# Two-layer streaming encoder: the second layer's conditioning rows are summed in the stage of the first output projection, and their order is changed

## The chip, the cores and the metric

The kernel runs on one core of one Trainium2 chip. The metric is device microseconds of one execution, here the median of three: 1983.85 us, from 1979.78 to 1991.28. One execution was also profiled. It took 1989.06 us, and the profile's span, from its first to its last instruction, is 1987.3 us.

Five engines work side by side, each through its own queue in the order in which its instructions were recorded: TensorE (PE in the profile, PEld for its weight loads), VectorE (DVE), ScalarE (ACT), GpSimd (POOL) and SyncE (SP). SP issues every DMA of this kernel. An instruction that must wait holds up everything behind it on the same queue.

## The reference, cut to what matters

Two layers work on a sequence of 2048 frames of width 1024. Layer 0 mixes with an RG-LRU block, layer 1 with a gated DeltaNet. Each is conditioned by three rows of 1024 numbers, shift, scale and gate, which are sums over the rows of a 1024 x 3072 matrix, weighted by one activated vector:

```python
c_act = jax.nn.silu(c)
for i in range(DEPTH):
    cond = c_act @ ada_w[i] + ada_b[i]
    shift = cond[:, None, :D_MODEL]
    scale = cond[:, None, D_MODEL:2 * D_MODEL]
    gate = cond[:, None, 2 * D_MODEL:]
    h = rmsnorm(x, norm_g[i]) * (1.0 + scale) + shift
    ...
    x = x + gate * out
return rmsnorm(x, final_g)
```

A mixer begins with a wide projection of h and ends with an output projection to `out`. So layer 1's shift and scale are needed when its normed input is made, after layer 0's output projection; layer 1's gate is needed at the very end.

## The kernel before

**Stages.** Frames are cut into two units of 1024 (NU), each into two tiles of 512 (NTC) and each tile into four blocks of 128. The program goes through: the projections of layer 0 (called `in1`, two units of 32 jobs) with the convolution, gates and scan of the RG-LRU beside them; the output projection of layer 0 (`out1`, 16 blocks by two halves, 32 jobs); the projections of layer 1 (`in2`, two units) with the DeltaNet beside them; and the output projection of layer 1. A job is 24 matmuls of 128x128 by 128x512 into one bank (`products`, line 663): each operand is split into a high and a low part, and three products are added for each of eight slices.

**What sets the order.** The program is written by generators ("threads"), and a planner, `Weave`, steps them: a thread asks for an engine for an estimated time, for a buffer (`slots`), or for an event, and the planner lets the one go first that can start earliest, with the smaller priority number ahead at equal times. The order of its choices is the order on each queue of the chip. A buffer class hands its buffers out in turn: with two buffers of class `tt`, the third request waits until the first has been given back.

**The rows.** The first four half rows of layer 0's shift and scale are made at the start of the program. The other eight half rows, layer 0's gate and all of layer 1, are made by `row_halves_thread` (line 397). For each half row it takes one of two `tt` buffers as an accumulator, and then four times: takes one of two `raw` buffers (which the weight panels also use), issues a DMA of 512 KB (line 408, tile `araw`), and adds its two 128x512 halves on VectorE (lines 413 and 415). TensorE then sums the accumulator over the partitions into a bank `adapt`: four one-column matmuls for shift and scale (`columns_of`, line 283, then `finish_columns`, lines 274 and 277), or one 128x512 matmul for a gate (line 426), to which a row of `ada_b` is added; layer 1's gate is written to memory for later (line 443). The list of half rows, (layer, part, half) with part 0 shift, 1 scale and 2 gate, is given on line 1643, and at the end the event `gates` is set.

**Who needs them.** `split_thread` (line 559) makes one slice of the normed input: ScalarE applies scale and shift (line 565), VectorE rounds to the high part (573), VectorE or GpSimd makes the low part (579, 576). It waits for `cond` of its layer. `panels_thread` loads the third weight panel of `in2` only after `gates` (line 622).

**The output projection of layer 0.** For each job, `residual1_thread` (line 919) waits for a tile `xr` of x loaded by `xr_thread` (line 932, issued on line 939, two buffers), multiplies the bank by the gate (923), adds (925) and writes the result to `x1_d` (928; the profile calls it `x_d`). Only when that write has landed is the buffer loaded again. `y_thread` (883) loads and splits one block of the mixer's result for every two jobs.

**The turn.** Beside these jobs the first two tiles of layer 1's input are turned, eight blocks in all: `turned_thread` (520) loads a block of `x1_d` (530), `scale_thread` (448) squares it on ScalarE into a `tt` buffer (455) and scales it, `turn_thread` (503) transposes it on VectorE (509) and writes it to `xt_d` in eight DMAs (515). When all eight are written, `reload_thread` (545) brings them back as `xk` (550), eight DMAs of 512 KB, and the splits of `in2` begin.

Of the kernel before, what the change touches and what calls it, by code (L numbers as in the profile page):

```python
# [138 lines left out]
def trunk_kernel(ctx, tc, x, c, ada_w, ada_b, ada_c, norm_c, final_g, w1, cw1, cb1, gate_w, gate_b, lam, ow1,  # L139
# [91 lines left out]
    def tile_(shape, tag, name, dtype=F32):  # L231
        p, n = tags[tag]
        return pools[p].tile(shape, dtype, tag=tag, name=name, bufs=n)

    w = Weave()
    events = {}

    def ev(*key):
        return events.setdefault(key, Event())

    def put(tag, token):
        w.put(slots[tag], token)
# [154 lines left out]
    def row_halves_thread(parts):  # L397

        row = tile_([P, D], "g1", "gate0")
        yield ev("gw", 0, 2)  # L400
        for layer, part, d in parts:
            ttok = yield slots["tt"]
            acc = tile_([P, TC], "tt", "acc")
            for q in range(4):
                wtok = yield slots["raw"]
                yield "sp", 512 * KB
                raw = tile_([P, 2, TC], "raw", "araw")
                sp.dma_start(out=raw, in_=ada_w[layer, 2 * part + d, :, 2 * q:2 * q + 2, :])
                for k in range(2):
                    ck = c_col[:, 2 * q + k:2 * q + k + 1]  # L410
                    yield "dve", STT, 0.13
                    if q + k == 0:
                        dve.tensor_scalar(acc, raw[:, 0, :], ck, None, ALU.mult)
                    else:
                        dve.scalar_tensor_tensor(acc, raw[:, k, :], ck, acc, ALU.mult, ALU.add)  # L415
                put("raw", wtok)
            ptok = yield slots["tp"]
            yield "pe", 0.86
            pt = ps.tile([P, TC], F32, tag="tp", name="adapt")
            if part < 2:  # L420
                columns_of(acc, pt)
                put("tt", ttok)
                yield from finish_columns(layer, part, d, pt[:, 0:4])
                put("tp", ptok)
                continue
            pe.matmul(pt, lhsT=ones, rhs=acc, start=True, stop=True)
            if layer == 0:
                put("tt", ttok)
                sl = row[:, d * TC:(d + 1) * TC]
                n = P  # L430
            else:
                sl = acc[0:1, :]
                n = 1
            yield "sp", 256 * KB
            j = 2 * part + d
            sp.dma_start(out=sl, in_=ada_b[layer:layer + 1, j * TC:(j + 1) * TC].to_broadcast([n, TC]))
            yield "dve", 0.61
            dve.tensor_tensor(sl, pt[0:n, :], sl, ALU.add)
            put("tp", ptok)
            w.set(ev("gate", layer, d), row)  # L440
            if layer == 1:
                yield "sp", 2 * KB
                sp.dma_start(out=gate_d[:, d * TC:(d + 1) * TC], in_=sl)
                put("tt", ttok)
        w.set(ev("gates"))
# [1183 lines left out]
    with tc.manual_schedule():  # L1629
        enter("hc", "o1", "l1")  # L1630
        ada_s = tile_([P, 2, 2, KT], "ada", "ada_s")
        norm_s = tile_([P, 2, KT], "ng", "norm_s")
        in1, in2 = [("in1", u) for u in range(NU)], [("in2", u) for u in range(NU)]
        w.spawn(first_small_thread(), 0)
        w.spawn(norm_thread((in1[0], 0), 0, x, 0, "A", [], [], htag="tg"), 1)
        w.spawn(first_loads_thread(), 1)
        w.spawn(first_pe_thread(), 1)
        w.spawn(first_dve_thread(), 0)
        w.spawn(columns_thread(), 4)
        w.spawn(panels_thread(), 1)  # L1640
        w.spawn(project_thread(), 9)
        w.spawn(lru_thread(), 4)
        w.spawn(row_halves_thread([(0, 2, 0), (0, 2, 1), (1, 0, 0), (1, 0, 1), (1, 1, 0), (1, 1, 1), (1, 2, 0),
                                   (1, 2, 1)]), 8)
        w.spawn(rows_thread(), 4)
        w.spawn(norm_thread((in1[0], 1), 0, x, TC, "B", [ev("adaissue", 3)], [ev("cond", 0, 1, 0), ev("cond", 0, 0, 0)],
                            ("yh", "yh", "yl", "yl")), 2)
        w.spawn(turned_thread((in1[1], 0), 0, x, T, "C", [ev("adaissue", 3), ev("split", (in1[0], 1), KT - 1)],
                              [ev("turned", (in1[1], 1))], [ev("ada")]), TP)
        w.spawn(turned_thread((in1[1], 1), 0, x, T + TC, "A", [ev("turned", (in1[1], 0))], [ev("loaded", (in1[1], 0))], [ev("free", in1[0], 0)]), TP)  # L1650
        w.spawn(out_weights_thread(1, ow1, 0, 0.5, "B", [ev("free", in1[0], 1)], []), 3)
        w.spawn(out_weights_thread(1, ow1, 1, 0.5, "C", [ev("w", *last[1])],
                                   [ev("free", in1[1], 0)]), 3)
        w.spawn(y_thread(), 3)
        w.spawn(xr_thread(), 3)
        w.spawn(phase1_end_thread(), 0)
        x1 = [[ev("x1", q * TB + b, d) for b in range(TB) for d in range(2)] for q in range(S // TC)]
        w.spawn(turned_thread((in2[0], 0), 1, x1_d, 0, "A", x1[0], [ev("turned", (in2[0], 1))],
                              [ev("free", in1[1], 1)]), TP)
        w.spawn(turned_thread((in2[0], 1), 1, x1_d, TC, "B", x1[1] + [ev("turned", (in2[0], 0))],  # L1660
                              [ev("loaded", (in2[0], 0))], [ev("free", "out1", 0)]), TP)
        w.spawn(turned_thread((in2[1], 0), 1, x1_d, T, "A", [ev("blkload", 0, BLK)],
                              [ev("blkload", 0, NH - 1), ev("turned", (in2[1], 1))], [ev("free", in2[0], 0)]), TP)
        w.spawn(turned_thread((in2[1], 1), 1, x1_d, T + TC, "B", [ev("turned", (in2[1], 0))],
                              [ev("loaded", (in2[1], 0))], [ev("free", in2[0], 1)]), TP)
        w.spawn(heads_thread(), 0)
        w.spawn(out_weights_thread(2, ow2, 0, onorm_s, "A", [ev("w", *last[-1])],
                                   [ev("free", in2[1], 0)]), 3)
        w.spawn(out_weights_thread(2, ow2, 1, onorm_s, "B", [ev("owissue", 2, 0)],
                                   [ev("free", in2[1], 1)]), 3)  # L1670
        w.spawn(queries_end_thread(), 0)
        w.spawn(phase2_end_thread(), 0)
        w.spawn(o_loads_thread(), 3)
        w.spawn(xt_thread(), 3)
        w.run()
        early.close()
        phase.close()
# [61 lines left out]
```

## Time and profile before

| what | value |
|---|---|
| median of three runs | 1983.85 us (1979.78 to 1991.28) |
| the profiled execution, its span | 1989.06 us, 1987.3 us |
| TensorE busy | 1869.0 us, 94% of the span |
| VectorE busy | 1500.0 us, 75% |
| ScalarE, GpSimd busy | 1025.1 us (52%), 811.3 us (41%) |
| DMA | 314.33 MB, mean 158 GB/s, queue 55.5% busy |
| first and last `araw` load | issued at 115.7 and 483.5 us |

The profile is read by stage. The first matmul of `out1` runs at about 518 us, the first one of `in2` at 701 us; the stage of the first projections lies before, and everything of layer 1 behind. A view that cuts the span into windows gives for each engine the busy time and the number of instructions, then the clock granted to TensorE as a share of full speed, the mean busy share of the 16 DMA engines and GB/s.

### The profile page before, as it was taken

Reading aid. Unit: us, or ns where it says so; the run is one execution under the profiler, and the core shown is the slowest. Engines: PE = TensorE matmul, PEld = TensorE weight load, DVE = VectorE, ACT = ScalarE, POOL = GpSimd, SP = SyncE. Lnnn points to the kernel's source line nnn. Section 1 sums busy time; section 2 is a strip of 40 time slices with the busy share of each in tenths; the row PEclk is TensorE's granted clock in tenths of the full one; section 3 lists DMA queues with packets and bytes.
Section 4 is the critical chain, followed back from the end, with each engine's and each line's share of the span. In section 5 each row is a group of like instructions: output and inputs, shape, how many; then the busy total and the mean of one; then the engine's idle time right before and its main releaser. Section 6 shows DMA issues by size and latency. Waiting matters only on the chain.

```text
span 1987.3 us, 31679 instructions
## 1 busy us (share of the span) xinstructions
PE 1869.0 (94%) x10408; PEld 1520.6 (77%) x10408; DVE 1500.0 (75%) x3176; ACT 1025.1 (52%) x2453; POOL 811.3 (41%) x1439
## 2 busy tenths in 40 slices
PE   6998889999999999999998989999999999999998
PEld 3776667787787777777777777788888888878887
DVE  6788798887644566888888897778777778877654
ACT  3655567666411225455555655555655556655321
POOL 4555664444200146555555553364343335511101
PEclk9999999999999999999999999999999999999999
DMA  8355655654578724546764447455455445577751
GB/s 333 97 159 160 220 169 171 199 170 156 172 199 206 223 63 127 136 111 160 177 161 126 107 115 187 135 125 146 114 129 142 120 127 128 142 208 233 224 185 64
DMA packets 506957, 314.33 MB, mean 158 GB/s; under 512 B 370724, under 2 KB 438564, under 8 KB 506792
## 3 DMA queue, kind: packets, MB, share of 16 engines
q1 hardware_dynamic: 506792, 312.31, 55.5%
q8 instruction: 82, 1.34, 0.3%
q14 instruction: 83, 0.68, 0.1%
HBM read 211.54 MB, written 100.67 MB: 157 GB/s over the span
## 4 chain that ended last, share of the span: by engine, by line
PE 50%; DVE 20%; DMA 10%; POOL 6%; issue 5%; ACT 5%; SPq 4%; DVEq 0%; POOLq 0%; ACTq 0%
PE mm L670 25%; PE mmo L670 12%; DVE xf L718 5%; DVE tblk L1248 2%; DVE ttmp L1245 2%; PE pg L777 2%; SPq L515 1%; DMA raw<-in_w 1%; DMA pq<-q_d 1%; DVE acc L415 1%; PE pp L1365 1%; PE py L1382 1%; DMA ada<-in_ada_w 1%; PE pS L1394 1%; PE pS L1395 1%
## 5 line engine op out<-in xcount | busy, mean ns | idle before, releaser
L718 DVE SCALAR_TENSOR_TENSOR xf<-xe,cw_s,xf 128x512 f32<-128x512 f32 x384 | 327.8, 855 | 54.9 <-POOL xf L961 32.0
L652 POOL TENSOR_TENSOR wlo<-raw,whi 128x1024 fp32r<-128x1024 f32 x48 | 122.3, 2548 | 81.0 <-ACT whi L646 67.9
L733 POOL COPY carry<-xe 128x4 f32<-128x4 f32 x128 | 36.8, 287 | 249.3 <-ACT xe L730 248.4
L1245 DVE TENSOR_TENSOR ttmp<-blk,tblk 128x60 f32<-128x60 f32 (+24 forms) x496 | 121.9, 246 | 21.0 <-DMA blk<-blk_d 11.0
L1248 DVE TENSOR_TENSOR tblk<-tblk,ttmp 128x60 f32<-128x60 f32 (+24 forms) x496 | 127.3, 257 | 10.1
L646 ACT CAST whi<-raw 128x1024 fp32r<-128x1024 f32 x96 | 100.3, 1045 | 52.8 <-DMA raw<-in_w 43.5
L730 ACT COPY xe<-mm 128x512 f32<-128x512 f32 x128 | 74.1, 580 | 78.6 <-PE mm L670 77.8
L670 PE MATMUL mmo<-oh,yh 128*128 128x512 f32 x256 | 102.2, 399 | 7.3 <-DVE xr L925 6.2
L670 PE MATMUL mm<-hh_('in2', 0)_5430,wlo 128*128 128x512 f32 x256 | 105.1, 411 | 0.0
L670 PE MATMUL mm<-hl_('in2', 0)_5431,whi 128*128 128x512 f32 x256 | 105.1, 410 | 0.0
L670 PE MATMUL mm<-hl_('in2', 1)_12333,whi 128*128 128x512 f32 x256 | 104.8, 409 | 0.0
L670 PE MATMUL mm<-hh_('in2', 0)_5430,whi 128*128 128x512 f32 x256 | 104.4, 408 | 0.0
L670 PE MATMUL mm<-hh_('in2', 1)_12332,wlo 128*128 128x512 f32 x256 | 104.3, 408 | 0.0
L670 PE MATMUL mm<-hh_('in2', 1)_12512,wlo 128*128 128x512 f32 x256 | 104.1, 407 | 0.0
L670 PE MATMUL mm<-hl_('in2', 0)_5208,whi 128*128 128x512 f32 x256 | 103.6, 405 | 0.0
L670 PE MATMUL mm<-hh_('in2', 0)_5207,whi 128*128 128x512 f32 x256 | 103.4, 404 | 0.2 <-ACT xe L730 0.2
L670 PE MATMUL mm<-hh_('in2', 0)_5207,wlo 128*128 128x512 f32 x256 | 103.5, 404 | 0.0
L670 PE MATMUL mm<-hh_('in2', 1)_12512,whi 128*128 128x512 f32 x256 | 103.5, 404 | 0.0
L670 PE MATMUL mm<-hl_('in2', 1)_12513,whi 128*128 128x512 f32 x256 | 103.2, 403 | 0.0
L670 PE MATMUL mm<-hh_('in2', 1)_12332,whi 128*128 128x512 f32 x256 | 103.1, 403 | 0.0
L670 PE MATMUL mmo<-oh,yl 128*128 128x512 f32 x256 | 101.7, 397 | 1.3 <-DVE yl L899 1.3
L670 PE MATMUL mmo<-oh,oh 128*128 128x512 f32 (+1 forms) x264 | 102.1, 387 | 0.0
(325 smaller groups left out, 5857.8 us busy)
## 6 DMA issues: line engine op xcount, KB each, us to landing
raw<-in_w SPq DMA_DIRECT2D x96, 512.0 KB, 4.3
araw<-in_ada_w SPq DMA_DIRECT2D x32, 512.0 KB, 4.6
xt<-x_d SPq DMA_DIRECT2D x32, 512.0 KB, 5.1
xt_d<-xb SPq DMA_DIRECT2D x192, 64.0 KB, 2.2
xk<-xt_d SPq DMA_DIRECT2D x24, 512.0 KB, 6.1
xt<-in_x SPq DMA_DIRECT2D x16, 512.0 KB, 5.1
ada<-in_ada_w SPq DMA_DIRECT2D x16, 512.0 KB, 9.0
y_d<-tz SPq DMA_DIRECT2D x32, 256.0 KB, 3.0
```

Source lines behind the costliest of these rows:

```text
L415: dve.scalar_tensor_tensor(acc, raw[:, k, :], ck, acc, ALU.mult, ALU.add)
L515: sp.dma_start(out=dst[c_], in_=tb[32 * c_:32 * c_ + 32])
L646: act.copy(hi, raw)
L652: pool.tensor_tensor(lo, raw, f(hi), ALU.subtract)
L670: pe.matmul(pt, lhsT=lhs[a][:, k, :], rhs=rhs[b][:, k, :], start=(k == 0 and n == 0), stop=(k == KT - 1 and n == 2))
L718: dve.scalar_tensor_tensor(xf, xe[:, 1 + j:1 + j + TC], wc[:, j:j + 1], xf, ALU.mult, ALU.add)
L730: act.copy(xe[:, 4:4 + TC], pt)
L733: pool.tensor_copy(out=carry, in_=xe[:, TC:TC + 4])
L777: pe.matmul(pg, lhsT=a[:, g, :], rhs=b, start=(q == 0), stop=(q == 2))
L1245: dve.tensor_tensor(tmp, blk[:, j, j + 1:32].unsqueeze(2).to_broadcast([P, r, c_]), t[:, j, 0:c_].unsqueeze(1).to_broadcast([P, r, c_]), A ...
L1248: dve.tensor_tensor(t[:, j + 1:32, 0:c_], t[:, j + 1:32, 0:c_], tmp, ALU.subtract)
L1365: pe.matmul(pp[:, 0, :], lhsT=kc, rhs=S_, start=True, stop=True)
```

## The change

Before the first half row of layer 1, `row_halves_thread` waits for the event `lasthalves`, which `gates_thread` sets (line 765) when the last of the 32 gate steps of the RG-LRU has its buffers, about where `out1` begins. And layer 1's half rows are taken in another order: shift and scale of the first 512 columns, then those of the second, then the gate.

```diff
@@ -399,6 +399,8 @@
         row = tile_([P, D], "g1", "gate0")
         yield ev("gw", 0, 2)
         for layer, part, d in parts:
+            if layer == 1:
+                yield ev("lasthalves")
             ttok = yield slots["tt"]
             acc = tile_([P, TC], "tt", "acc")
             for q in range(4):
@@ -1640,7 +1642,7 @@
-        w.spawn(row_halves_thread([(0, 2, 0), (0, 2, 1), (1, 0, 0), (1, 0, 1), (1, 1, 0), (1, 1, 1), (1, 2, 0),
+        w.spawn(row_halves_thread([(0, 2, 0), (0, 2, 1), (1, 0, 0), (1, 1, 0), (1, 0, 1), (1, 1, 1), (1, 2, 0),
                                    (1, 2, 1)]), 8)
```

No instruction is added or taken away; every queue holds as many as before. Lines behind 402 stand two further down in the changed kernel (line 415 is 417 there, 925 is 927, and so on). What the planner makes of it is seen in the order of the queues.

**SP, late in the first projections.** Names: `raw` is a weight panel, `wlo` a kept low part read back, `y_d` a result written, `gw` gate weights. Before:

```order
L819 DMA y_d<-tz 128x512
L408 DMA araw<-in_ada_w 128x1024
L837 DMA gw<-in_gate_w 128x256
L408 DMA araw<-in_ada_w 128x1024
L610 DMA raw_3102<-in_w 128x1024
L641 DMA wlo<-wlo_d1z_1261 128x1024
L408 DMA araw<-in_ada_w 128x1024
L819 DMA y_d<-tz 128x512
```

and now, at the same two panels:

```order
L821 DMA y_d<-tz 128x512
L839 DMA gw<-in_gate_w 128x256
L612 DMA raw_3051<-in_w 128x1024
L643 DMA wlo<-wlo_d1z_1261 128x1024
L821 DMA y_d<-tz 128x512 x2
```

All 24 `araw` loads of layer 1 have left this stage.

**VectorE, in the first jobs of the output projection.** `mmo` is the job's bank, `yl` the low part of a mixer block. Before, four jobs read:

```order
L923 TENSOR_TENSOR mmo<-mmo,gate_138 128x512
L925 TENSOR_TENSOR xr<-mmo,xr 128x512
L899 TENSOR_TENSOR yl<-yf,yh 128x1024
L923 TENSOR_TENSOR mmo<-mmo,gate_138 128x512
L925 TENSOR_TENSOR xr<-mmo,xr 128x512
L923 TENSOR_TENSOR mmo<-mmo,gate_138 128x512
L925 TENSOR_TENSOR xr<-mmo,xr 128x512
L923 TENSOR_TENSOR mmo<-mmo,gate_138 128x512
L925 TENSOR_TENSOR xr<-mmo,xr 128x512
```

and now:

```order
L925 TENSOR_TENSOR mmo<-mmo,gate_138 128x512
L927 TENSOR_TENSOR xr<-mmo,xr 128x512
L274 TENSOR_TENSOR cond<-adapt,ada_s 128x4
L415 TENSOR_SCALAR acc<-araw,c_col 128x512
L417 SCALAR_TENSOR_TENSOR acc<-araw,c_col,acc 128x512
L925 TENSOR_TENSOR mmo<-mmo,gate_138 128x512
L927 TENSOR_TENSOR xr<-mmo,xr 128x512
L417 SCALAR_TENSOR_TENSOR acc<-araw,c_col,acc 128x512 x2
L925 TENSOR_TENSOR mmo<-mmo,gate_138 128x512
L901 TENSOR_TENSOR yl<-yf,yh 128x1024
L927 TENSOR_TENSOR xr<-mmo,xr 128x512
```

Two sums of a loaded tile now stand between the residual of one job and that of the next. On SP the load that they need is issued between the two writes of `x_d`, behind the next load of `xr`.

**VectorE, where the output projection ends and `in2` begins.** `hh` and `hl` are the high and low part of a slice of layer 1's input, `xb` is a turned block. Before, ten rows that begin with the residual of the 25th of the 32 jobs:

```order
L923 TENSOR_TENSOR mmo<-mmo,gate_138 128x512
L925 TENSOR_TENSOR xr<-mmo,xr 128x512
L573 CAST hh_('in2', 0)_5207<-h 128x512
L579 TENSOR_TENSOR hl_('in2', 0)_5208<-h,hh_('in2', 0)_5207 128x512
L573 CAST hh_('in2', 0)_5207<-h 128x512 x2
L579 TENSOR_TENSOR hl_('in2', 0)_5208<-h,hh_('in2', 0)_5207 128x512
L573 CAST hh_('in2', 0)_5207<-h 128x512 x2
L923 TENSOR_TENSOR mmo<-mmo,gate_138 128x512
L579 TENSOR_TENSOR hl_('in2', 0)_5208<-h,hh_('in2', 0)_5207 128x512
L925 TENSOR_TENSOR xr<-mmo,xr 128x512
```

and now, with the residuals of the last two jobs:

```order
L511 STREAM_TRANSPOSE xb<-xt 128x512
L925 TENSOR_TENSOR mmo<-mmo,gate_138 128x512
L927 TENSOR_TENSOR xr<-mmo,xr 128x512
L417 SCALAR_TENSOR_TENSOR acc<-araw,c_col,acc 128x512 x2
L511 STREAM_TRANSPOSE xb<-xt 128x512
L925 TENSOR_TENSOR mmo<-mmo,gate_138 128x512
L927 TENSOR_TENSOR xr<-mmo,xr 128x512
L440 TENSOR_TENSOR acc<-adapt,acc 1x512
L575 CAST hh_('in2', 0)_5439<-h 128x512
L581 TENSOR_TENSOR hl_('in2', 0)_5440<-h,hh_('in2', 0)_5439 128x512
```

The last block is turned only between the last two residuals, and the sixteen splits of `in2` all stand behind the last one. On SP the eight `xk` loads stand behind the last write of `x_d`; before, the first of them stood ahead of the last eight.

## Prediction

> **What bounds the kernel now.** I read the page's engine shares first, then windows by stage, then the waits and rows of the two stages that the change touches.
>
> ```profile
> PE 1869.0 (94%) x10408; PEld 1520.6 (77%) x10408; DVE 1500.0 (75%) x3176; ACT 1025.1 (52%) x2453; POOL 811.3 (41%) x1439
> ```
>
> TensorE is busy for 94% of the span, so a gain must come out of the remaining 6%, or out of matmuls that run slowly. The windows say where these are. Columns: window, length, PE, PEld, DVE, ACT, POOL, granted clock, DMA share, GB/s.
>
> ```profile
> 255.00:310.00 55.00, 47.40 (x190) 37.14 (x191) 49.64 (x65) 37.32 (x51) 33.19 (x29) 0.91 0.50 158
> 310.00:400.00 90.00, 86.01 (x376) 69.78 (x375) 75.24 (x94) 62.17 (x82) 38.48 (x44) 0.98 0.60 196
> 400.00:490.00 90.00, 89.21 (x391) 72.00 (x390) 75.12 (x97) 63.35 (x82) 39.15 (x46) 1.00 0.52 171
> 490.00:518.00 28.00, 26.27 (x112) 20.66 (x111) 21.55 (x22) 14.21 (x18) 12.73 (x12) 1.00 0.41 132
> 518.00:560.00 42.00, 41.97 (x184) 34.16 (x183) 20.73 (x25) 10.91 (x12) 2.96 (x3) 1.00 0.53 178
> 560.00:610.00 50.00, 46.88 (x201) 37.49 (x200) 24.31 (x33) 8.81 (x12) 3.15 (x8) 0.99 0.82 208
> 610.00:660.00 50.00, 47.23 (x200) 37.50 (x199) 23.34 (x32) 8.70 (x12) 3.22 (x8) 0.98 0.85 212
> 660.00:701.00 41.00, 38.30 (x157) 31.07 (x156) 24.66 (x38) 14.61 (x18) 9.55 (x7) 0.92 0.61 216
> ```
>
> The row 518 to 560 is TensorE undisturbed: 184 matmuls in 42 us, 0.228 us each, a job of 24 in 5.47 us. Against that pace the four rows of the first projections lose 55 - 190 x 0.228 = 11.7 us, then 4.3, 0.9 and 2.5, together **19.4 us**. 32 of the counted matmuls are one-column ones (below), which are cheaper than 0.228 by 3 us in all, so at most 22 can go. The output projection, 518 to 701, already loses about 13, nearly all of it behind 560, where the DMA share is above 0.8. VectorE has room there: half busy, against 90% in the first row.
>
> **What is taken out of the first projections.** Columns of the next view: min/median/max ns, first and last start.
>
> ```profile
> L415 DVE SCALAR_TENSOR_TENSOR acc<-araw,c_col,acc x56: 711/747/2264, 130.2 to 489.4; 128x512 f32<-128x512 f32 x56
> L408 SPq DMA_DIRECT2D araw<-in_ada_w x32: 327/346/918, 115.7 to 483.5; - x32
> ...
> DMA to landing us min/median/max: 3.4/4.6/7.3
> ```
>
> ```profile
> L283 PE MATMUL adapt<-ones,acc x32: 166/250/271, 299.6 to 422.4; 128*128 128x1 f32 x32
> ...
> L426 PE MATMUL adapt<-acc,ones x8: 590/593/922, 167.4 to 492.5; 128*128 128x512 f32 x8
> ```
>
> Six of eight half rows move: 24 loads of 512 KB, 48 sums of about 0.75 us, 36 us of VectorE, and on TensorE four one-column groups of about 1.05 us and two full ones of 1.2, **6.6 us** together. These 6.6 leave one stage and return in the next: zero. What counts is who waited.
>
> ```profile
> PE pg L777 <- DVE xl L771: 8.7, 6, 5.2
> ...
> PE adapt L283 <- DVE acc L415: 3.5, 3, 1.7
> ...
> PE mm L670 <- ACT whi L646: 2.3, 1, 2.3
> ```
>
> ```profile
> 268.13 1.07 DVE L415 SCALAR_TENSOR_TENSOR acc<-araw,c_col,acc 128x512 f32<-128x512 f32 x1
> ...
> 277.06 2.55 DVE L415 SCALAR_TENSOR_TENSOR acc<-araw,c_col,acc 128x512 f32<-128x512 f32 x2
> ...
> 282.59 0.68 DVE L771 TENSOR_TENSOR xl<-xf,xh 128x512 fp32r<-128x512 f32 x1
> ```
>
> Between 255 and 518 TensorE waits 3.5 us for the sums themselves. Its longest wait, 5.2 us for `xl` at 283, has sums on VectorE just ahead of it, 1.07 + 2.55 us, and a single one between them. After it the clock is low:
>
> ```profile
> 280.00:300.00 20.00, 14.93 (x56) 11.35 (x57) 18.28 (x26) 15.61 (x21) 13.00 (x11) 0.83 0.52 164
> 300.00:320.00 20.00, 20.00 (x85) 16.43 (x85) 15.75 (x17) 13.77 (x18) 9.32 (x11) 0.91 0.41 124
> ```
>
> A clock of 0.83 over 20 us costs 3.4 us. So I take 8.5 of the 11.7 us of the first window (4.4 ahead of `xl`, 1.8 at the `adapt` group, the rest clock), 4 of 4.3 in the second (1.7 for sums; 2.3 for a weight panel that shares the two `raw` buffers), 0.5 and 1.5 in the last two: **-15 us**. Bounds: -5, the wait for sums and little else; -22, the whole loss.
>
> **What the output projection takes on.** DMA columns are KB each and median us to landing, in the window of this stage:
>
> ```profile
> x_d<-xr SPq DMA_DIRECT2D x32, 256.0 KB, 2.9
> xr<-in_x SPq DMA_DIRECT2D x31, 256.0 KB, 3.3
> yf<-y_d SPq DMA_DIRECT2D x13, 512.0 KB, 6.0
> xt<-x_d SPq DMA_DIRECT2D x8, 512.0 KB, 5.0
> xt_d<-xb SPq DMA_DIRECT2D x64, 64.0 KB, 3.1
> xk<-xt_d SPq DMA_DIRECT2D x8, 512.0 KB, 6.6
> ```
>
> ```profile
> 679.42 0.70 DVE L923 TENSOR_TENSOR mmo<-mmo,gate 128x512 f32<-128x512 f32 x1 [3.45 <-PE mmo L670]
> ...
> 681.65 0.68 DVE L925 TENSOR_TENSOR xr<-mmo,xr 128x512 f32<-128x512 f32 x1
> ```
>
> A residual writes `x_d`; when that has landed (2.9 us), SP issues the next `xr` (0.35) and right behind it the `araw` load, which lands L later; two sums (1.5) and then the residual two jobs on (1.4). The round takes 6.15 + L us; TensorE needs 10.94 for two jobs. So the loads are free up to L = 4.8. Before, the round ended with `xr`: 2.9 + 3.3 + 1.4, well inside. Queued behind a waiting sum on VectorE are the residual, which frees the bank, `yl`, which feeds the next block, and the turn.
>
> L in this stage is not in the trace. The bounds are the fastest load seen, 3.4 (no cost), and `xk` at 6.6 (1.8 us a round). 24 loads, with odd and even jobs going round side by side, are twelve rounds: 0 to 22 us. Nearest is `xt`, the same size and also whole rows, at 5.0; but 12.6 MB more in 183 us is 69 GB/s, which at the 178 GB/s for a share of 0.53 of the row from 518 adds 0.2 to a mean share of 0.72. I take L = 5.55, **+9 us**. The six `adapt` groups will wait for sums as before, about **+4** (0 to 8).
>
> The Trainium skill, DMA: Bandwidth & Descriptors, in its part on the fixed cost, fits one DMA as 2.0 us plus its bytes over 436 GB/s, measured on another kind of queue. That makes 3.2 us of a 512 KB load, below the 4.8, and +9 would become 0. This trace has 4.6 as the median of just these loads and 3.4 as the least, so I keep the row.
>
> **The handover to `in2`.** Before, TensorE goes over without a gap:
>
> ```profile
> 670.78 30.36 PE mmo L670 x120
> 701.14 9.29 PE mm L670 x41
> ```
>
> because the splits of the first tile were made from 663 on, beside the last residuals. Now they stand behind the last one, as `tt` explains: an accumulator keeps one of the two `tt` buffers for a whole half row, and as buffers go in turn, the turn's squares wait behind it. So the last block is turned between the last two residuals. What is late next is the split:
>
> ```profile
> L565 ACT ACTIVATE h<-xk,cond x16: 799/815/817, 662.2 to 700.0; 128x512 f32<-128x512 f32 x16
> ...
> DMA to landing us min/median/max: 3.6/6.6/9.1
> ```
>
> ```profile
> 663.07 0.43 DVE L573 CAST hh_('in2', 0)_5207<-h 128x512 fp32r<-128x512 f32 x1 [1.75 <-ACT h L565]
> ...
> 674.22 0.41 DVE L573 CAST hh_('in2', 0)_5207<-h 128x512 fp32r<-128x512 f32 x1
> ```
>
> From the end E of the last job: the last four `xt_d` writes are issued until about E + 1 and land 3.1 later, E + 4; `xk` lands 3.6 later on a queue with nothing ahead of it, E + 7.6; 0.8 on ScalarE. The eight splits took 11.6 us in the trace, 9 without the 2.6 us of other work between them, so the last is there at E + 17.5 and the job ends at E + 18.3, in place of E + 5.5: 12.8 us late. The next job uses the same slices, and the second tile's are made under it. A clock fall like the one at 283 adds 1 to 2. **+14 us**; from 8 (`xk` issued right away, splits at ScalarE's 0.8) to 20 (`xk` at 6.6, splits at 11.6). The third weight panel, issued beside `xk`, is needed only after four jobs, 22 us: no cost. The rest of layer 1 is TensorE's, so what is lost here stays lost.
>
> **The sum**: -15 + 9 + 4 + 14 = **+12 us**. Made against the profiled execution, 1989.06 us, that is 2001; this one lies 5.2 above the median of its runs, so beside 1983.85 it is **1996 us**.
>
> **Rivals.**
> - *The output projection falls into the round of loads.* L at 6.6 or more, as for `xk` and up to 7.3 at worst: +22 there, +8 at `adapt`, +16 at the handover, -15: +31, 2015 us. For it speaks the share of 0.85 that the stage has already; against it that `xr` keeps 3.3 there.
> - *Only moved.* L below 4.8, and the handover near its lower end: -15 + 4 + 0 + 9 = -2, 1982 us. For it: 518 to 560 has a share of 0.53 and VectorE half idle.
> - *Faster.* One mechanism: short landings. From L below 4.8 on, VectorE never stands before a sum, so neither residuals nor `adapt` groups wait; the first projections, freed of the same stalls, reach TensorE's own pace, -22, and the handover costs 9: -13, 1971 us. Against it: the median of 4.6 was had at shares of 0.5 to 0.6.
> - *The first projections don't get shorter.* Convolution, gates and scan hold VectorE anyway (50 of 55 us busy, eight of them sums): -5 in place of -15, +22, 2006 us.
>
> **How the numbers follow.** Forecast 0.43, with a range of its own from 1986 to 2006; the round of loads 0.20, only moved 0.22, faster 0.09, no shorter 0.06. A measurement tells about 0.5% from no change, 10 us. Slower by more than that: 0.29 of the forecast, 0.20 and 0.06, together 0.55. Within: 0.14 of it and 0.22, 0.36. Faster: 0.09. The range from 1975 to 2018 leaves out nearly all of the faster case and half of the round of loads.
>
> **What would show it.** Right: in the changed profile the windows of the first projections lose the low clock and some 15 us besides the moved 6.6; `araw` in the output projection lands in over 4.8 us and `xr` or `yl` name longer waits of TensorE; between the last `mmo` and the first full job of `in2` there is an idle time of about 9 us, ended by `hh` or `hl`. Wrong: if the first matmul of `in2` follows without a gap, if `out1` takes no longer than its 183 us plus 6.6, or if the first projections end no earlier.

## The result and the profile after

| | before | after |
|---|---|---|
| median of 18 runs each | 1983.85 us (1979.78 to 1991.28) | 1998.12 us (1988.69 to 2007.36) |
| profiled execution's span | 1987.3 us | 2002.4 us |
| mean granted clock | 0.981 | 0.977 |

The changed kernel takes **1.0072** times as long, with a 95% interval from 1.0059 to 1.0085: 14.3 us more. Both profiled executions lie above the median of their kernel, by 5.2 and 6.0 us. The page of the changed kernel shows the same work on every engine as before; a loss inside a stage can't be seen in it:

```profile
PE 1872.7 (94%) x10408; PEld 1523.3 (76%) x10408; DVE 1500.5 (75%) x3176; ACT 1023.6 (51%) x2453; POOL 799.8 (40%) x1439
```

So the time has to be found by stage. The rows of one tile, here the bank `mmo`, give the shortest, median and longest ns of a matmul and then its first and last start. Product `oh,yh` belongs to the output projection of layer 0, `oh,oh` to that of layer 1. Before:

```profile
L670 PE MATMUL mmo<-oh,oh x264: 278/389/501, 1792.6 to 1979.7; 128*128 128x512 f32 x124, 128*128 128x256 f32 x8
...
L670 PE MATMUL mmo<-oh,yh x256: 387/389/793, 507.5 to 700.3; 128*128 128x512 f32 x128
```

And after:

```profile
L672 PE MATMUL mmo<-oh,oh x264: 277/389/501, 1807.7 to 1994.8; 128*128 128x512 f32 x124, 128*128 128x256 f32 x8
...
L672 PE MATMUL mmo<-oh,yh x256: 389/389/796, 496.6 to 701.5; 128*128 128x512 f32 x128
```

The medians are equal: the matmuls have not changed, their places have. The output projection really begins at 507.5 us before; the 518 that the sections ahead use is where TensorE runs on undisturbed. With one more mark, the 97th matmul of `in2` (the start of its fifth job, at 732.6 before and 747.6 after), the 15.1 us between the two spans fall into four pieces:

| stage, in the profiled executions | before, us | after, us | difference |
|---|---|---|---|
| start to the first matmul of `out1` | 507.5 | 496.6 | -10.9 |
| `out1`, first matmul to the end of the last | 193.6 | 205.7 | +12.1 |
| from there to the fifth job of `in2` | 31.5 | 45.3 | +13.8 |
| from there to the first matmul of the last output projection | 1060.0 | 1060.1 | +0.1 |

The +0.1 of the last piece is partly chance: in the profiles of the other kernels below, the same piece takes from 1049.7 to 1058.9 us.

**The first projections.** The windows of the changed kernel, with the columns of the prediction's:

```profile
255.00:310.00 55.00, 50.93 (x206) 40.88 (x207) 47.69 (x59) 38.76 (x53) 34.24 (x30) 0.94 0.46 150
310.00:400.00 90.00, 85.89 (x363) 69.64 (x362) 66.62 (x77) 65.77 (x88) 35.67 (x46) 0.96 0.41 131
400.00:490.00 90.00, 89.68 (x393) 73.47 (x392) 64.64 (x70) 61.39 (x82) 34.00 (x47) 1.00 0.36 116
490.00:518.00 28.00, 23.93 (x103) 18.88 (x101) 22.33 (x24) 15.69 (x19) 11.43 (x9) 1.00 0.59 204
518.00:560.00 42.00, 40.95 (x181) 33.74 (x182) 26.04 (x36) 4.21 (x4) 2.12 (x2) 0.96 0.69 220
560.00:610.00 50.00, 47.16 (x210) 38.15 (x209) 27.59 (x40) 7.66 (x10) 2.23 (x6) 1.00 0.80 222
610.00:660.00 50.00, 43.93 (x181) 35.08 (x179) 27.19 (x39) 6.39 (x8) 1.48 (x4) 0.90 0.85 246
660.00:701.00 41.00, 38.56 (x164) 30.75 (x165) 24.54 (x36) 5.56 (x8) 2.46 (x6) 1.00 0.86 230
701.00:760.00 59.00, 48.90 (x204) 34.59 (x202) 42.27 (x74) 23.16 (x35) 25.17 (x30) 0.91 0.39 126
```

Against 0.228 us for a matmul the first row loses 55 - 206 x 0.228 = 8.0 us where it lost 11.7, but the second now loses 7.2 where it lost 4.3. What TensorE waited for between 255 and 507 (total, times, longest), where `pg` is the bank of the RG-LRU's gates, `xl` the low part of what is multiplied for them, `mm` the bank of a projection and `xe` its copy, made by ScalarE:

```profile
PE pg L779 <- DVE xl L773: 8.4, 5, 2.9
PE mm L672 <- ACT xe L732: 3.7, 1, 3.7
...
```

The last of the waits for `xl`, 1.4 us, lies behind the first matmul of `out1` here. Up to that matmul they come to 7.0 us, and to 7.3 in the kernel before: the wait of 5.2 us has broken up into smaller ones with nearly the same total. The waits for sums, 3.5 us, are gone, and the wait for `xe` is new. ScalarE shows where it comes from (start, us, idle time before it and who ended it):

```profile
306.10 1.06 ACT L879 ACTIVATE oh<-oraw 128x1024 fp32r<-128x1024 f32 x1 [4.09 <-DMA oraw<-in_ow]
```

ScalarE stands before a tile of output weights (`oraw`, whose high part is `oh` and low part `ol`) that is still on its way, with the copies that free TensorE's banks behind it.

**The output projection.** What TensorE waited for from 496 to 712:

```profile
PE mm L672 <- DVE hh_('in2', 0)_5439 L575: 8.1, 1, 8.1
PE mmo L672 <- DVE xr L927: 5.1, 2, 4.6
PE adapt L283 <- DVE acc L417: 2.8, 3, 1.3
PE adapt L428 <- DVE acc L417: 2.5, 2, 1.4
PE mmo L672 <- ACT oh L879: 2.1, 1, 2.1
...
PE mmo L672 <- DVE ol L881: 0.9, 1, 0.9
...
```

And before, from 507 to 701:

```profile
PE mmo L670 <- DVE xr L925: 6.2, 4, 2.7
```

The `adapt` groups wait 5.3 us for their sums and are 6.6 us of work, together 11.9 us, nearly the whole 12.1. The rest about cancels: the waits for output weights, 3.0 us and all in the first four jobs, are new, and those for residuals and `yl` are 1.9 us shorter. The loads themselves, from the rows of `araw` between 500 and 712, with VectorE's idle time before its sums (us, times):

```profile
L410 SPq DMA_DIRECT2D araw<-in_ada_w x23: 328/430/972, 512.9 to 694.1; - x23
...
  DMA araw<-in_ada_w: 32.2, 16
...
DMA to landing us min/median/max: 3.7/4.7/9.1
```

**The handover.** TensorE's timeline where `out1` ends:

```profile
701.94 0.39 PE L672 MATMUL mmo<-oh,yl 128*128 128x512 f32 x1
710.44 0.80 PE L672 MATMUL mm<-hh_('in2', 0)_5439,whi 128*128 128x512 f32 x1 [8.11 <-DVE hh_('in2', 0)_5439 L575]
...
714.73 0.63 PE L672 MATMUL mm<-hh_('in2', 0)_5439,wlo 128*128 128x512 f32 x1
```

And the window behind the idle time, with the columns as above:

```profile
710.00:716.00 6.00, 5.52 (x11) 3.23 (x12) 5.05 (x10) 3.39 (x5) 2.56 (x2) 0.50 0.98 359
```

An idle time of 8.11 us, and then a slow start: the first 21 matmuls of `in2` take 9.6 us, where 4.8 would do at 0.228 us each. The granted clock is 0.50 up to 716, which is 11 x 0.2 = 2.2 us of the loss. The rest is waiting for splits, 0.73 us of it in one piece at 718.

### The profile page after: what moved, and what is told of

It reads as the page before. It is cut to its first block, busy times and chain, and to the rows that moved or that the text cites. A ratio compares the mean times of both kernels' runs of the same rounds, so it can differ in the third digit from the quotient of the medians.

```text
span 2002.4 us, 31678 instructions
## 1 busy us (share of the span) xinstructions
PE 1872.7 (94%) x10408; PEld 1523.3 (76%) x10408; DVE 1500.5 (75%) x3176; ACT 1023.6 (51%) x2453; POOL 799.8 (40%) x1439
## 4 chain that ended last, share of the span: by engine, by line
PE 51%; DVE 18%; DMA 11%; issue 7%; POOL 5%; ACT 5%; SPq 3%; DVEq 0%; POOLq 0%; ACTq 0%
PE mm L672 28%; PE mmo L672 10%; DVE xf L720 4%; DVE tblk L1250 2%; PE pg L779 2%; DMA raw<-in_w 2%; DVE ttmp L1247 2%; DMA araw<-in_ada_w 2%; DMA xt<-x_d 1%; DMA x_d<-xr 1%; PE pkk L1127 1%; PE pS L1396 1%; SPq L1185 1%; PE pS L1397 1%; PE pp L1367 1%
## 5 line engine op out<-in xcount | busy, mean ns | idle before, releaser
L672 PE MATMUL mm<-hh_('in2', 0)_5439,whi 128*128 128x512 f32 x256 | 106.3, 415 | 8.8 <-DVE hh_('in2', 0)_5439 L575 8.1
L672 PE MATMUL mm<-hl_('in2', 0)_5440,whi 128*128 128x512 f32 x256 | 105.2, 411 | 0.8 <-POOL hl_('in2', 0)_5440 L578 0.7
L672 PE MATMUL mm<-hh_('in2', 0)_5463,whi 128*128 128x512 f32 x256 | 105.1, 411 | 0.3 <-DVE tz L991 0.3
L672 PE MATMUL mm<-hh_('in2', 0)_5439,wlo 128*128 128x512 f32 x256 | 105.2, 411 | 0.0
L672 PE MATMUL mm<-hh_('in2', 0)_5463,wlo 128*128 128x512 f32 x256 | 105.0, 410 | 0.0
L672 PE MATMUL mm<-hl_('in2', 1)_12356,whi 128*128 128x512 f32 x256 | 104.9, 410 | 0.0
L672 PE MATMUL mm<-hl_('in2', 0)_5464,whi 128*128 128x512 f32 x256 | 104.4, 408 | 0.0
L672 PE MATMUL mm<-hh_('in2', 1)_12513,whi 128*128 128x512 f32 x256 | 103.8, 405 | 0.0
L672 PE MATMUL mm<-hh_('in2', 1)_12513,wlo 128*128 128x512 f32 x256 | 103.6, 405 | 0.0
L672 PE MATMUL mm<-hh_('in2', 1)_12355,wlo 128*128 128x512 f32 x256 | 103.6, 405 | 0.0
```

Of the source, the lines that this page charges most:

```text
L672: pe.matmul(pt, lhsT=lhs[a][:, k, :], rhs=rhs[b][:, k, :], start=(k == 0 and n == 0), stop=(k == KT - 1 and n == 2))
```

## The experiments

Each ratio is against the kernel before, timed on the same chip beside it. The kernels ran 4 to 12 times each, in three groups on three chips (e1 to e4, e5 to e8, e9 to e12). Stage marks are those of the table above, one profiled execution each. Single executions of one kernel lie up to 9 us to either side of its median, and marks and ratios do not add up to better than 7 us: e5 reaches the fifth job 1.2 us earlier than the kernel before and is 0.3%, 6 us, slower. So a mark tells where time went in one execution, and only the ratio tells what a kernel costs.

| kernel | median, us | ratio, 95% interval | `out1` begins | `out1` takes | to the fifth job of `in2` |
|---|---|---|---|---|---|
| e1_order | 1986.75 | 1.0020 (1.0006 to 1.0034) | 507.9 | 195.5 | 31.5 |
| e2_wait | 1994.78 | 1.0059 (1.0039 to 1.0080) | 496.1 | 206.9 | 45.2 |
| e3_ownsq | 1991.24 | 1.0039 (1.0022 to 1.0055) | 497.3 | 213.9 | 32.4 |
| e4_none | 1977.90 | 0.9975 (0.9961 to 0.9989) | 500.0 | 190.2 | 31.5 |
| e5_oneload | 1988.74 | 1.0030 (1.0017 to 1.0042) | 497.8 | 202.1 | 31.5 |
| e6_ownsq_later | 2027.64 | 1.0227 (1.0211 to 1.0242) | 497.4 | 205.3 | 76.1 |
| e7_mid | 1992.92 | 1.0052 (1.0037 to 1.0068) | 504.1 | 203.9 | 31.5 |
| e8_noadapt | 2003.13 | 1.0104 (1.0089 to 1.0119) | 497.5 | 199.1 | 49.6 |
| e9_owlater | 1999.66 | 1.0083 (1.0067 to 1.0099) | 492.1 | 212.9 | 45.1 |
| e10_nosums | 1987.28 | 1.0029 (1.0016 to 1.0043) | 495.9 | 210.2 | 32.4 |
| e11_owlater_before | 1987.29 | 1.0024 (1.0013 to 1.0035) | 507.2 | 192.2 | 31.5 |
| e12_nosums_before | 1975.78 | 0.9969 (0.9957 to 0.9981) | 500.3 | 190.1 | 31.5 |

### Which half of the change counts

**e1_order** is the kernel before with the new order of half rows and no wait:

```diff
-        w.spawn(row_halves_thread([(0, 2, 0), (0, 2, 1), (1, 0, 0), (1, 0, 1), (1, 1, 0), (1, 1, 1), (1, 2, 0),
+        w.spawn(row_halves_thread([(0, 2, 0), (0, 2, 1), (1, 0, 0), (1, 1, 0), (1, 0, 1), (1, 1, 1), (1, 2, 0),
```

> The new order of the half rows alone, on the kernel before, without the wait; nothing is left out. If the stage in which the sums run is what counts, this is the time of before within 0.3%, and TensorE goes from the output projection to in2 without a gap. If the order matters, some of the 14 us appear here.

**e2_wait** is the changed kernel with the old order:

```diff
-        w.spawn(row_halves_thread([(0, 2, 0), (0, 2, 1), (1, 0, 0), (1, 1, 0), (1, 0, 1), (1, 1, 1), (1, 2, 0),
+        w.spawn(row_halves_thread([(0, 2, 0), (0, 2, 1), (1, 0, 0), (1, 0, 1), (1, 1, 0), (1, 1, 1), (1, 2, 0),
```

> The wait alone, with the old order of the half rows; nothing is left out. Theory: the time of the changed kernel, 10 to 18 us above before, with the same idle time of about 8 us of TensorE ahead of in2. Rival, the order is part of the cost: under 5 us above before.

The order alone costs 0.2%; the wait alone gives all three stages of the changed kernel within 1.2 us, with an idle time of 8.02 us at the handover, and a ratio that overlaps the change's. So the place is the main cost; the order adds little.

### What the half rows cost where they stood

**e4_none** is the kernel before without layer 1's loads and sums, and without the matmuls for its gate:

```diff
-            for q in range(4):
+            if layer == 1 and part < 2:
+                put("tt", ttok)
+                yield from finish_columns(layer, part, d, ones[:, 0:4])
+                continue
+            for q in range(0 if layer == 1 else 4):
                 wtok = yield slots["raw"]
...
+            if layer == 1:
+                j = 2 * part + d
+                yield "sp", 256 * KB
+                sp.dma_start(out=acc[0:1, :], in_=ada_b[layer:layer + 1, j * TC:(j + 1) * TC])
+                yield "sp", 2 * KB
+                sp.dma_start(out=gate_d[:, d * TC:(d + 1) * TC], in_=acc[0:1, :])
+                put("tt", ttok)
+                continue
```

> The half rows of layer 1 are left out: no loads, no sums, no matmuls for them; shift, scale and gate of layer 1 get only ada_b. So it gives the price of the half rows at either place. Theory: 10 to 15 us below before, since the first projections end about 11 us earlier, as they do in the changed kernel, and the output projection takes no longer than before. If the sums cost the first projections more than the changed kernel won back, it is 20 us or more below; if they cost nothing there, it is before within 0.3%.

Leaving all of it out gains 0.25%, 5 us. `out1` begins only 7.5 us earlier, though the 6.6 us of TensorE's own work are gone as well, so there was never much to win by moving the half rows. The planner makes another order without them, and part of the gain is lost in it: TensorE has a new wait of 4.5 us for `xe`, as in the changed kernel. So e4 shows what this planner makes of their absence, and not the price of each part.

**e12_nosums_before** separates the sums from the rest. All loads and `adapt` groups stay at their old place, but 42 of the 48 sums work on 8 of the 512 columns:

```diff
-                        dve.scalar_tensor_tensor(acc, raw[:, k, :], ck, acc, ALU.mult, ALU.add)
+                        m = 8 if layer == 1 else TC
+                        dve.scalar_tensor_tensor(acc[:, 0:m], raw[:, k, 0:m], ck, acc[:, 0:m], ALU.mult, ALU.add)
```

> The same cut of the sums on the kernel before, with its order and loads: VectorE's work of the sums alone is taken out of the first projections. My prediction's working (up to 15 us of TensorE's waits there hang on the sums) wants the first matmul of out1 at about 495 us and 10 us or more off the time. Rival, after what leaving all out has shown: the work of other engines takes the place at once, out1 begins within 4 us of 507.5 and the time is within 0.3% of before.

`out1` begins 7.2 us earlier and the time falls by 0.31%, as much as with everything left out. So the sums on VectorE account for all of the gain that was to be had; what the loads and the `adapt` groups cost beside them can't be told from zero. The queues are those of the kernel before, so its longest wait can be followed. In the kernel before, and in e12:

```profile
283.32 0.80 PE L777 MATMUL pg<-xl,gh 128*128 128x512 f32 x1 [5.16 <-DVE xl L771]
```

```profile
280.47 0.79 PE L778 MATMUL pg<-xl,gh 128*128 128x512 f32 x1 [2.75 <-DVE xl L772]
```

The three sums ahead of it fell from 4.4 to 1.2 us, and the wait from 5.16 to 2.75. So 2.4 us of it hung on the sums, where the prediction took 4.4, and VectorE's other work sets the rest. All waits for `xl` between 255 and 507 fall from 7.3 us to this:

```profile
PE pg L778 <- DVE xl L772: 5.6, 6, 2.8
```

By the pace of 0.228 us the first window loses 6.2 us (214 matmuls in 55 us) in place of 11.7, the second 3.6 (379 in 90) in place of 4.3.

### Why the first projections gained less

**e9_owlater** and **e11_owlater_before** take away the new wait, that for the output weights. The loads of output weights share the two `raw` buffers with the half rows; in the changed kernel the first half of them, four loads, was issued from 288 to 311 us in place of 294 to 336. Both kernels hold this half back until an event late in the second unit, to about 400 us, e9 on the changed kernel and e11 on the one before:

```diff
-        w.spawn(out_weights_thread(1, ow1, 0, 0.5, "B", [ev("free", in1[0], 1)], []), 3)
+        w.spawn(out_weights_thread(1, ow1, 0, 0.5, "B", [ev("free", in1[0], 1), ev("gw", 1, 4)], []), 3)
```

> The changed kernel, with the first half of layer 0's output weights loaded later, when the fifth gate block of the second unit is ready; nothing is left out. In the changed kernel ScalarE stands 4.1 us at 306 us before such a load and TensorE waits 3.7 us behind it. Theory, part of what the first projections should have won went to these loads, which took the freed raw buffers too early: that wait goes, out1 begins 3 to 6 us earlier than at 496.6 us, and the time falls by 3 to 6 us. Rival, VectorE's order of convolution, gates and scan holds the stage: out1 begins within 2 us of 496.6.

> The same later load of the output weights on the kernel before; nothing is left out. If these loads collide with the weight panels in the raw buffers there as well (a wait of 2.3 us at 334 us), it gains 2 to 4 us and beats both kernels; else it is before within 0.3%.

In e9 the wait for `xe` is gone, and `out1` begins at 492.1, another 4.5 us earlier. It brings nothing:

```profile
L672 PE MATMUL mmo<-oh,yh x256: 387/389/796, 492.1 to 704.1; 128*128 128x512 f32 x128
```

The output projection takes 212.9 in place of 205.7 us and ends 2.7 us later than in the changed kernel. The ratios of the two overlap. In the kernel before (e11) the same edit costs 0.24%. The head start is gone by the 67th matmul of `out1`, which waits for the second half of the output weights. In the changed kernel, and in e9:

```profile
516.98 0.50 PE L672 MATMUL mmo<-oh,yh 128*128 128x512 f32 x1 [2.14 <-ACT oh L879]
```

```profile
517.06 0.80 PE L672 MATMUL mmo<-oh,yh 128*128 128x512 f32 x1 [4.29 <-ACT oh L879]
```

The last load of these weights is issued at 510.7 and 510.2 us, so an earlier beginning only waits longer here.

### The handover

By the prediction's reasoning the squares of the turn wait behind an accumulator for a `tt` buffer. **e3_ownsq** gives these squares a buffer of class `th`, which the gates no longer use there:

```diff
-    def scale_thread(xt, done):
+    def scale_thread(xt, done, tag="tt"):
...
-        ttok = yield slots["tt"]
+        ttok = yield slots[tag]
...
-        yield from scale_thread(xt, ev("scaled", key, b))
+        yield from scale_thread(xt, ev("scaled", key, b), "th" if key[0] == ("in2", 0) else "tt")
```

> The changed kernel, but the turn of the first two tiles of layer 1 squares its blocks into a buffer of the class th, idle by then, so it does not stand in turn behind the accumulators. Theory, the handover costs 14 us because the accumulators hold the tt buffers: the first split comes before the last residual, the idle time ahead of in2 is gone, and the time falls by 10 to 14 us, to before within 0.3%. Rival, the handover is late because loads and sums make the output projection's queues late: the idle time stays over 5 us and the time falls by under 4 us.

The rows of the squares `sqj` between 600 and 720 (ns, then first and last start), in the kernel before, the changed kernel and e3:

```profile
L455 ACT ACTIVATE sqj<-xt x4: 1057/1058/1059, 614.8 to 641.6; 128x1024 bf16<-128x1024 f32 x4
```

```profile
L457 ACT ACTIVATE sqj<-xt x5: 1056/1057/1059, 621.9 to 693.1; 128x1024 bf16<-128x1024 f32 x5
```

```profile
L457 ACT ACTIVATE sqj<-xt x4: 1052/1056/1057, 619.4 to 652.4; 128x1024 bf16<-128x1024 f32 x4
```

The last block was squared at 641.6 before, at 693.1 with the change, and at 652.4 with a buffer of its own. The gap goes with it: the first matmul of `in2` follows the last of `out1` at once, and the third mark is back at 32.4. So the shared buffer was the cause, as predicted. But the time falls from 1.0072 to 1.0039 only, some 6.5 of the 13.8 us, as the output projection takes 213.9 us in place of 205.7. What e3's TensorE waited for from 497 to 745:

```profile
PE adapt L283 <- DVE acc L417: 6.3, 2, 3.5
...
PE adapt L428 <- DVE acc L417: 2.5, 1, 2.5
```

The turn's transfers now run in the same stage as the half rows' (241 GB/s from 518 to 700, 231 in the changed kernel), and the `adapt` groups wait 8.8 us rather than 5.3.

### Loads, sums or matmuls: what holds the output projection

**e5_oneload** is e3 with 18 of layer 1's 24 loads left out; its sums run four times on the first tile of each half row:

```diff
-                wtok = yield slots["raw"]
-                yield "sp", 512 * KB
-                raw = tile_([P, 2, TC], "raw", "araw")
-                sp.dma_start(out=raw, in_=ada_w[layer, 2 * part + d, :, 2 * q:2 * q + 2, :])
+                if layer == 0 or q == 0:
+                    wtok = yield slots["raw"]
+                    yield "sp", 512 * KB
+                    raw = tile_([P, 2, TC], "raw", "araw")
+                    sp.dma_start(out=raw, in_=ada_w[layer, 2 * part + d, :, 2 * q:2 * q + 2, :])
...
-                put("raw", wtok)
+                if layer == 0 or q == 3:
+                    put("raw", wtok)
```

> On the kernel with the squares in th (e3_ownsq, whose output projection took 213.9 us against 193.6 before). Each half row of layer 1 loads only its first 512 KB and sums it four times: 18 of 24 loads are left out, all sums and adapt matmuls stay. Theory, the output projection is long because loads land late under a busy queue, so sums, adapt groups and residuals wait: it falls to 200 us plus or minus 3 and the time by 8 to 14 us against e3_ownsq. Rival, VectorE's 36 us of sums and TensorE's own 6.6 us make it long: it falls by under 4 us.

**e10_nosums** is e3 with the sums cut to 8 columns by the diff of e12.

> On e3_ownsq, order and loads unchanged, but of each sum of layer 1 only the first 8 of 512 columns are made (the first of a half row in full), so nearly 36 us of VectorE are left out and all DMAs stay. Theory, the output projection (213.9 us there) is long for its loads: it stays within 4 us, VectorE waits for araw as long. Rival, VectorE's sums make it long: 8 us or more go.

In the profiled executions the loads weigh more: without them `out1` takes 202.1 us (-11.8), without the sums 210.2 (-3.7). The times don't confirm that: 1.0030 and 1.0029 against e3's 1.0039, all three overlapping. The profiled execution of e3 lay 3.5 us above its median and that of e5 3.6 below, which is 7 of the 9.6 us between their spans. What the pair does show is that leaving out neither the loads nor the sums alone takes away e3's loss. e10 and e12 differ by the place of the half rows, their order and e3's buffer: without the sums, and without the gap, the new place still costs 0.6%.

**e8_noadapt** is the changed kernel without the `adapt` matmuls and the bias of layer 1:

```diff
+            if layer == 1 and part < 2:
+                yield from finish_columns(layer, part, d, acc[:, 0:4])
+                put("tt", ttok)
+                continue
             ptok = yield slots["tp"]
...
-            pe.matmul(pt, lhsT=ones, rhs=acc, start=True, stop=True)
             if layer == 0:
+                pe.matmul(pt, lhsT=ones, rhs=acc, start=True, stop=True)
```

> The changed kernel without the adapt matmuls of layer 1 and the bias behind them: loads and sums stay, shift, scale and gate are taken from the accumulator as it is. Theory, what the output projection gained in length, 12.1 us, is these groups: their own 6.6 us and TensorE's 5.3 us of waits for sums; it falls to 194 us plus or minus 3, and the handover keeps its idle time of about 8 us, so the time falls by about 12 us. Rival, the loads' round holds the output projection: it falls by 7 us or less.

`out1` takes 6.6 us less, and the idle time behind it grows from 8.11 to 12.54:

```profile
709.14 0.79 PE L678 MATMUL mm<-hh_('in2', 0)_5422,whi 128*128 128x512 f32 x1 [12.54 <-DVE hh_('in2', 0)_5422 L581]
```

TensorE's work there is cover, not cost: `in2` starts at 709.1, only 1.3 us earlier, since its start is set by the last turned block: its writes are issued until about 702.7 us here and until 703.9 in the changed kernel. The time is 1.0104, even above the change's, while the profiled execution is 2.5 us shorter than the changed kernel's. Why the time is not below I can't say from these runs; e8 ran only four times.

**e6_ownsq_later** is e3 with the sums planned 3 us later, so that VectorE would not stand before a load still on its way:

```diff
                 sp.dma_start(out=raw, in_=ada_w[layer, 2 * part + d, :, 2 * q:2 * q + 2, :])
+                if layer == 1:
+                    yield "none", 3.0
```

> On e3_ownsq, with the planner told to place each sum of layer 1 3 us later behind its load; nothing is left out. Theory, the waits come from sums that stand on VectorE and TensorE ahead of their load's landing: VectorE's waits for araw (20.9 us) and TensorE's for sums (8.8 us) fall to under half, the output projection by 6 to 12 us. Rival, the DMA queue as a whole is short (share 0.9): the waits move to other loads and the projection changes by under 4 us.

VectorE's idle time before sums fell from 23.2 us to 5.4, and the kernel became 2.3% slower. The half rows run on past the end of `out1`, and with them the event `gates`, which holds the third panel of `in2` back. SP's timeline (start, us of issue):

```profile
754.17 0.33 SPq L410 DMA_DIRECT2D araw<-in_ada_w  x1
...
771.49 0.23 SPq L447 DMA_DIRECT2D gate_d<-acc  x1
771.76 0.36 SPq L614 DMA_DIRECT2D raw<-in_w  x1
```

The panel is asked for 0.3 us after the gate row is written, and TensorE is idle for most of that time:

```profile
740.00:780.00 40.00, 13.63 (x40) 9.24 (x40) 22.17 (x54) 11.46 (x32) 12.12 (x26) 0.51 0.27 74
```

In the changed kernel the last load is issued at 694.1 and the gate row written at 704.6; the panel follows at 706.3 and costs nothing. The condition behind "no cost" is that the half rows end by the handover.

### A place between

**e7_mid** waits for a half-way point of the second unit (about 350 us) in place of `lasthalves`:

```diff
             if layer == 1:
-                yield ev("lasthalves")
+                yield ev("gw", 1, 2)
```

> The changed kernel, but layer 1's half rows may start when the third gate block of the second unit is ready, at about 350 us, in place of about 500; nothing is left out. VectorE and the queue have room there and TensorE lost only 0.9 us of 90 in the window from 400 with the sums in it. Theory, the cost of the change is the output projection and the handover: with most loads back in the first projections the time is that of before within 0.3%, at best 4 us below, the price of the half rows that leaving them out showed. Rival, any delay of the half rows costs: 5 us or more above before.

The last half rows still reach into the output projection, their loads until 554 us; `out1` begins 3.4 us earlier than before and takes 10.3 us longer. No `adapt` group waits there. The loss lies in the first four jobs, 36.8 us in place of 25.4; the other 28 take 167.1 in place of 168.2. TensorE's waits from 504 to 541:

```profile
PE mmo L672 <- ACT oh L879: 3.6, 2, 2.7
PE mmo L672 <- DVE ol L881: 2.1, 3, 0.8
...
```

These are output weights again, of which the kernel before waits for none: their second half is loaded from 492 to 526 us in place of 490 to 514, while the half rows take the same `raw` buffers just there. In the changed kernel the same waits are 3.0 us and the first four jobs take 30.0. Both delays that were run cost time.

No kernel that computes everything beat the kernel before. e4 and e12 put what was to be won at 5 to 6 us, 8.5 at the far end of an interval; as the planner orders e4 anew, that is an estimate and not a strict bound.

## Why the prediction came out right

The time predicted was 2.1 us off, with the sign right, but two of its four terms were wrong by 10.7 and 9 us and offset each other. That the number came out so close is luck: with only one of the two put right, the sum would have been +23 or +3 us. The direction does not hang on it.

| term of the sum | predicted, us | the profile shows, us |
|---|---|---|
| first projections, besides the 6.6 of work moved | -15 | -10.9 + 6.6 = -4.3 |
| output projection, round of loads | +9 | 0 |
| output projection, waits of `adapt` | +4 | +5.3 |
| handover | +14 | +13.8 |
| sum | +12 | +14.8; the spans differ by 15.1 |

- **First projections: the step that failed.** The working took 8.5 of the 11.7 us lost in the first window and 4 of 4.3 in the second. It took 4.4 of the 5.2 us wait for `xl` to go with the sums ahead of it. e12 cuts just the sums: this wait falls by 2.4 us, the waits for `xl` in all from 7.3 to 5.6, and the whole stage by 7.2 us, 0.31% of the time, which is half of the 15. In the changed kernel even that was not had: the order of VectorE's queue is another, with 7.0 us of waits for `xl`, and the freed `raw` buffers were not left idle but taken early by output weights, with a new wait of 3.7 us for which the sum had no term. e9 shows the price of that wait, 4.5 us at this mark, and that removing it brings no time, as TensorE then waits longer for the second half of the weights. The rival "the first projections don't get shorter" had -5 for this stage and was nearer than the forecast; its reason, that VectorE is held there anyway, is half of the story by e12.
- **Round of loads: nothing came of it.** The working took L = 5.55 against a break-even of 4.8 us; the loads landed in 4.7 in the median, and the waits for residuals went from 6.2 to 5.1 us. That does not show the formula to be right. The landings, from 3.7 to 9.1 us, lie on both sides of the break-even, and VectorE did stand before sums, 16 times and 32.2 us in all. In e3 the loads landed in 5.2 us in the median between 518 and 700; twelve rounds of 5.2 - 4.8 would make about 5 us of longer waits, and the waits for residuals are 1.7 us there. VectorE's standing reached TensorE through the `adapt` groups instead. The Trainium skill, DMA: Bandwidth & Descriptors, in its part on the fixed cost, would have made this term 0 by an estimate of 3.2 us for 512 KB from its fit. The 0 came about, but not by that number: these loads took 4.7 us in the median and 3.7 at least.
- **Waits of `adapt`**: 5.3 for 4, inside the bounds.
- **Handover: right in size and cause.** The idle time was 8.11 us for "about 9", ended by `hh`, and the first 21 matmuls took 9.6 us, partly at a clock of 0.50 (about 2 us, for the 1 to 2 of the working) and partly for the splits. e3 removes the cause and the gap. Only the belief that each of these microseconds is worth its own length was untested: e3 returned half.
- **Third panel: "no cost"** held, but only because the half rows ended before it; e6 shows the price of that condition, 1.0227 against e3's 1.0039, or 37 us.

What stays open is how the cost of e3 and e10, 0.39 and 0.29% over the kernel before, divides between loads, waiting `adapt` groups and the clock; two experiments aimed at it gave times too close together. Also open is why e8, with less work, is not faster than the change.

## What to carry to other kernels

Work that stands beside a busy engine may be nearly free where it is: leave it out once (e4, e12) before moving it, as that gives an estimate of the most that can be won. When work moves, follow what it shares, here two classes of two buffers and an event that releases a panel, and ask who takes the buffers it gives up and who must wait for those it now holds. A long wait with removable work just ahead of it need not go with that work: here 2.4 of 5.2 us did. And shortening a stage pays only if nothing behind it waits for something else anyway, as `out1` did for its last weights.

## What the runs showed of the hardware

**Some waits cost about twice what the list of waits shows.** TensorE's timeline in e3:

```profile
610.68 1.55 PE L283 MATMUL adapt<-ones,acc 128*128 128x1 f32 x8 [2.78 <-DVE acc L417]
612.10 0.77 PE L672 MATMUL mmo<-oh,yl 128*128 128x512 f32 x1
612.67 0.63 PE L672 MATMUL mmo<-oh,yh 128*128 128x512 f32 x1
...
617.37 0.60 PE L672 MATMUL mmo<-oh,yl 128*128 128x512 f32 x1
617.79 0.41 PE L672 MATMUL mmo<-oh,yh 128*128 128x512 f32 x1
```

After the wait of 2.78 us thirteen matmuls start 0.43 us apart in place of 0.228, the window from 611 to 616 has a granted clock of 0.50, and 13 x 0.2 = 2.6 us are lost again. In the changed kernel a wait of 4.55 us for a residual, from 622 on, is followed by the same: 0.50 from 628 to 634. Over 518 to 700 the granted clock is 0.97 before, 0.96 with the change and 0.95 in e3, about 1.8 us for each step. The Trainium skill, TensorE: Matmul & The Clock Gate, in its section on what is actually happening, has the clock fall to half after at least one idle window of about 3.4 us. The waits of 4.55 us, and of 8.11 us at the handover with 0.50 behind it, are longer, and the trace agrees. The 2.78 us alone are shorter; with the one-column matmuls behind them, from 607.9 to 612.1, it is 4.2 us, so this place agrees if such a group counts as idle, and no run here separates the two.

**Landing times did not rise together with the load.** In the window 518 to 700 the mean DMA share rose from 0.72 to 0.81. Rows of the DMA issues of the changed kernel, KB each and median us to landing:

```profile
araw<-in_ada_w SPq DMA_DIRECT2D x22, 512.0 KB, 4.7
xr<-in_x SPq DMA_DIRECT2D x29, 256.0 KB, 3.3
...
yf<-y_d SPq DMA_DIRECT2D x13, 512.0 KB, 4.8
xt<-x_d SPq DMA_DIRECT2D x8, 512.0 KB, 6.5
```

Against the rows of the prediction `xr` kept its 3.3 us, `yf` fell from 6.0 to 4.8 and `xt` rose from 5.0 to 6.5, so the mean share alone did not tell how long a load takes. The working had let `araw` rise with it.
